# One row's load in three parts of 112, 8 and 8 partitions in a log-sum-exp kernel

## The chip, the core and the metric

The kernel runs on one core of one Trainium2 chip. A core has a matrix engine (PE), VectorE (DVE), ScalarE (ACT), GpSimd (POOL) and SyncE (SP), and 16 DMA engines that move data between the chip's main memory (HBM) and the on-chip memory of 128 partitions. The metric is the device time of one execution in microseconds (us); the number given for a kernel is the median of its runs.

## The reference

```python
def setup_inputs():
    batch, seq, dim = 32, 512, 1024
    return {"x": np.random.randn(batch, seq, dim).astype(np.float32), "axis": -1}

def reference(x, axis):
    x_max = np.max(x, axis=axis, keepdims=True)
    return (x_max.squeeze(axis) + np.log(np.sum(np.exp(x - x_max), axis=axis))).astype(np.float32)
```

For each of 32 x 512 = 16384 vectors of 1024 numbers it gives the logarithm of the sum of the exponentials. The input has 67.11 MB, the output 0.07 MB.

## The kernel before

**Tiles.** The 16384 vectors are laid out as 128 partitions with 128 vectors each: partition p holds the vectors 128p to 128p + 127. The kernel calls one vector per partition, that is 128 vectors of 4 KB, 512 KB together, a *row*; there are 128 rows. Rows are held in `ring`, a buffer of 51 rows; later rows take the places of earlier ones.

**First pass.** The exponentials are taken without subtracting the maximum. At the end the kernel checks that no sum of the rows left a safe range (`bounds`, `above`, `votes`, `verdict`, lines 283 to 312); only if one did, a second pass does the whole thing again with the maximum subtracted. With this input the second pass is not taken.

**Chunks and the order of the work.** The order is written out by hand in `CHUNKS`, a list of 17 chunks: 4, 15, 16, 16, 16, 14, 13, 9, 7, 5, 4, 3, 2, 1, 1, 1, 1 rows. Chunk `i` is loaded by `load(i)` and has its own semaphore `landed[i]`. Of each chunk, ScalarE takes the exponentials of the first `n_dve` rows in one or two instructions (line 235), and VectorE sums each row (line 255, or line 242 by halves); the other rows are done on ScalarE alone, one instruction a row, which exponentiates and sums at once (line 262, and line 225 for the last row). The last four chunks have one row each, the rows 124 to 127, all on ScalarE alone. Ahead of the last row ScalarE takes the logarithm of the sums of the rows 81 to 123 (line 162), after it that of the last four rows.

**Loads.** All loads are issued by SyncE, one after the other in the order of the chunks, onto one queue. A load waits until VectorE or ScalarE has finished with the rows of `ring` that it overwrites (`dve_wait`, `act_wait`). A load of all 128 partitions is one DMA instruction (line 155, line 146 for the last row). The waits in front of row 124 are for VectorE's sum over the rows that held its place; the loads of rows 124 to 127 are issued at 128.74, 129.12, 129.59 and 130.07 us of the profiled span, and wait in the DMA queue behind the earlier ones.

**The switch that the change uses.** `load` has a branch that splits a load by partitions. `UNEVEN` lists the chunks for which it is taken, and `PARTS` the parts: first partition, last partition, step. It is off in the kernel before (`UNEVEN` is empty). Each part adds 16 to the chunk's semaphore when it has landed, and ScalarE waits for 16 times the number of parts:

```python
nc.scalar.wait_ge(landed[i], 16 * (len(PARTS) if i in UNEVEN else 1))
```

Of the kernel before, what the change touches and what calls it, by code (L numbers as in the profile page):

```python
# [17 lines left out]
RING_ROWS = 51  # L18


UNEVEN = ()
PARTS = ((0, 128, 2), (1, 128, 4), (3, 128, 8), (7, 64, 8), (71, 128, 8))


LN_AT = 7
# [13 lines left out]
def kernel(  # L39
# [91 lines left out]
    def cuts(n, parts):  # L131
        ends = [-(-n * k // parts) for k in range(parts + 1)]
        return [(lo, hi) for lo, hi in zip(ends, ends[1:]) if lo < hi]

    def load(i):
# [8 lines left out]
        if i == len(CHUNKS) - 1:  # L144
            for k, (lo, hi) in enumerate(spans):
                nc.sync.dma_start(out=dst[:, :, lo:hi], in_=src[:, :, lo:hi]).then_inc(
                    landed[i + k], 16
                )
        elif i in UNEVEN:
            for first, last, step in PARTS:  # L150
                nc.sync.dma_start(
# [61 lines left out]
    for i, (r, n_dve, parts, by_halves) in enumerate(CHUNKS):  # L213
# [6 lines left out]
        if i == len(CHUNKS) - 1:  # L220
# [11 lines left out]
            continue  # L232
        nc.scalar.wait_ge(landed[i], 16 * (len(PARTS) if i in UNEVEN else 1))
        for lo, hi in cuts(n_dve, parts):
# [161 lines left out]
```

## Time and profile before

| | us |
|---|---|
| median of 3 runs | 162.54 |
| lowest and highest run | 162.43, 162.83 |
| the profiled execution | 162.67 |
| its span, first to last instruction | 161.3 |
| VectorE busy | 121.9 (76%) |
| ScalarE busy | 115.1 (71%) |
| mean rate of the DMA engines | 417 GB/s |

The span is what the profile's times are counted in, from the first instruction. The profile's page cuts it into 40 equal slices; a digit gives the busy share of an engine in a slice in tenths. The chain that ended last is read backwards from the last instruction, at each step to what released it. A line of the timeline gives start, duration, engine, source line, operation and shapes; where the engine stood idle before it, the idle time and what ended it follow in brackets. The issue of a DMA is an instruction of SyncE; "to landing" is the time from its issue to the last of its semaphore's counts. A load over all 16 DMA engines raises its semaphore sixteen times, once for each engine, and the trace records the time of each count.

### The profile page before, as it was taken

The page shows a single profiled execution, that of the slowest core. Times are in us where ns is not written, and L with a number is a line of the kernel's source. Part 1 is how long each engine was busy: PE and PEld are TensorE (multiplying, and loading weights), DVE is VectorE, ACT ScalarE, POOL GpSimd, SP SyncE. Part 2 cuts the span into 40 slices and gives each one's busy share as a digit, 9 for nine tenths or more (in the row PEclk, how much of TensorE's full clock was granted, in tenths as well). Part 3 has the DMA queues.
Part 4 walks back from the last instruction along what each step waited for, and adds up shares of the span by engine and source line. Part 5 has one row for each costly group of instructions (what it writes and reads, how often), then busy time and mean ns, then how long its engine had stood idle before and what let it go on. Part 6 is the DMA issues. An engine that isn't in the chain of part 4 may idle for free.

```text
span 161.3 us, 149 instructions
## 1 busy us (share of the span) xinstructions
PE 0.2 (0%) x2; PEld 0.1 (0%) x2; DVE 121.9 (76%) x51; ACT 115.1 (71%) x40; POOL 0.4 (0%) x8
## 2 busy tenths in 40 slices
PE   0000000000000000000000000000000000000000
PEld 0000000000000000000000000000000000000000
DVE  0028000003999999999999699999999999999884
ACT  3170005996079960999419993999199999999996
POOL 1000000000000000000000000000000000000000
DMA  7999799979979989989979999999999999999991
GB/s 256 508 488 442 305 472 520 439 341 520 439 341 520 423 358 520 423 358 520 423 325 455 455 455 439 423 423 423 412 402 430 436 420 410 427 436 412 417 407 42
DMA packets 2737, 67.18 MB, mean 417 GB/s; under 512 B 560, under 2 KB 560, under 8 KB 1072
## 3 DMA queue, kind: packets, MB, share of 16 engines
q1 hardware_dynamic: 2736, 67.18, 97.4%
q14 instruction: 1, 0.01, 0.0%
HBM read 67.11 MB, written 0.07 MB: 416 GB/s over the span
## 4 chain that ended last, share of the span: by engine, by line
DMA 49%; DVE 30%; ACT 20%; issue 0%; PE 0%
DMA ring<-in_x_dram 49%; DVE sums L255 29%; ACT ring L235 17%; ACT ring L262 3%; ACT ring L225 1%; ACT res L162 0%; DVE above L283 0%; PE votes L304 0%; DVE verdict L312 0%; PE votes L307 0%
## 5 line engine op out<-in xcount | busy, mean ns | idle before, releaser
L255 DVE TENSOR_REDUCE sums<-ring 128x8 f32<-128x8192 f32 (+5 forms) x14 | 111.2, 7994 | 37.3 <-ACT ring L235 37.2
L235 ACT ACTIVATE ring<-ring 128x8192 f32<-128x8192 f32 (+6 forms) x18 | 104.4, 5836 | 43.9 <-DMA ring<-in_x_dram 43.9
L242 DVE CUSTOM_DVE_ANT_0 ring<-ring 128x512 f32<-128x512 f32 x16 | 9.9, 684 | 0.0
L262 ACT ACTIVATE ring<-ring 128x1024 f32<-128x1024 f32 x8 | 8.2, 1041 | 0.0
L205 ACT ACT_TABLE_LOAD x1 | 1.3, 1283 | 0.8 <-PEq L377 0.8
L262 ACT ACTIVATION_READ_ACCUMULATOR ring<-ring 128x1 f32 x8 | 1.4, 174 | 0.0
L242 DVE DVE_READ_ACCUMULATOR2_ANT sums<- 128x1 f32 x16 | 1.3, 80 | 0.0
L225 ACT ACTIVATE ring<-ring 128x1024 f32<-128x1024 f32 x1 | 1.0, 1040 | 0.0
L283 DVE TENSOR_TENSOR above<-late,bounds 128x8 bf16<-128x8 f32 x1 | 0.2, 168 | 0.7 <-ACT res L162 0.7
L162 ACT ACTIVATE res<-sums 128x81 f32<-128x81 f32 (+1 forms) x2 | 0.5, 248 | 0.0
L312 DVE TENSOR_REDUCE verdict<-votes 1x1 int32<-1x6 f32 x1 | 0.2, 152 | 0.3 <-PE votes L307 0.3
L293 DVE TENSOR_REDUCE ends<-sums 128x1 f32<-128x124 f32 x1 | 0.3, 282 | 0.1
L304 PE MATMUL votes<-above,weights 128*1 128x6 bf16 x1 | 0.2, 167 | 160.0 <-DVE above L283 160.0
L294 DVE TENSOR_REDUCE ends<-sums 128x1 f32<-128x124 f32 x1 | 0.3, 271 | 0.0
L283 DVE TENSOR_TENSOR above<-ends,bounds 128x4 bf16<-128x4 f32 x1 | 0.2, 162 | 0.1
L162 ACT ACTIVATE res<-late 128x4 f32<-128x4 f32 x1 | 0.2, 173 | 0.0
L304 PEld LDWEIGHTS votes<-above,weights 128*1 128x1 bf16 x1 | 0.1, 80 | 160.0 <-DVE above L283 160.0
L307 PE MATMUL votes<-above,weights 128*1 128x6 bf16 x1 | 0.2, 165 | 0.0
L225 ACT ACTIVATION_READ_ACCUMULATOR ring<-ring 128x1 f32 x1 | 0.2, 153 | 0.0
L206 POOL MEMSET bounds<- 128x6 f32 x1 | 0.1, 104 | 0.4 <-POOLq L377 0.4
L207 POOL MEMSET bounds<- 128x6 f32 x1 | 0.1, 104 | 0.0
L377 POOL MEMSET const-bfloat16-1.0<- 128x1 bf16 x1 | 0.1, 103 | 0.0
(6 smaller groups left out, 0.6 us busy)
## 6 DMA issues: line engine op xcount, KB each, us to landing
ring<-in_x_dram SPq DMA_DIRECT2D x1, 7680.0 KB, 25.1
ring<-in_x_dram SPq DMA_DIRECT2D x1, 7168.0 KB, 28.6
ring<-in_x_dram SPq DMA_DIRECT2D x1, 6656.0 KB, 35.7
ring<-in_x_dram SPq DMA_DIRECT2D x1, 4608.0 KB, 20.3
ring<-in_x_dram SPq DMA_DIRECT2D x2, 2048.0 KB, 16.2
ring<-in_x_dram SPq DMA_DIRECT2D x1, 3584.0 KB, 28.5
ring<-in_x_dram SPq DMA_DIRECT2D x1, 2560.0 KB, 27.5
ring<-in_x_dram SPq DMA_DIRECT2D x4, 512.0 KB, 27.2
```

The costliest lines, as they stand in the source:

```text
L162: nc.scalar.activation(out=res[:, lo:hi], in_=src, func=Ln, bias=bias).then_inc(act_done, 1)
L205: nc.scalar.preload_act_table_set("natural_log_exp_and_others")
L225: nc.scalar.activation(out=ring[:, s, lo:hi], in_=ring[:, s, lo:hi], func=Exp, accum_out=late[:, LATE - 1 + k : LATE + k],).then_inc(act_d ...
L235: nc.scalar.activation(out=ring[:, s + lo : s + hi], in_=ring[:, s + lo : s + hi], func=Exp).then_inc(act_done, 1)
L242: nc.vector.tensor_tensor_reduce(out=ring[:, s + j, : D // 2], in0=ring[:, s + j, : D // 2], in1=ring[:, s + j, D // 2 :], scale=1.0, scal ...
L255: nc.vector.reduce_sum(out=sums[:, row + lo : row + hi], in_=ring[:, s + lo : s + hi], axis=AX).then_inc(dve_done, 1)
L262: nc.scalar.activation(out=ring[:, s + j], in_=ring[:, s + j], func=Exp, accum_out=total(row + j),).then_inc(act_done, 1)
L283: nc.vector.tensor_tensor(out=above[:, :, lo:hi], in0=values.unsqueeze(1).to_broadcast([P, 2, hi - lo]), in1=bounds[:, :, lo:hi], op=Alu.i ...
L293: nc.vector.reduce_max(out=ends[:, :1], in_=sums[:, :late_row], axis=AX).then_inc(dve_done, 1)
L294: nc.vector.tensor_reduce(out=ends[:, 1:], in_=sums[:, :late_row], axis=AX, op=Alu.min).then_inc(dve_done, 1)
L304: nc.tensor.matmul(votes[:1, :K], lhsT=weights[:, :1], rhs=above[:, 0], start=True, stop=False)
L307: nc.tensor.matmul(votes[:1, :K], lhsT=weights[:, 1:], rhs=above[:, 1], start=False, stop=True).then_inc(counted, 1)
```

## The change

The load of chunk 13, which is row 124, the fourth from last, is taken through the branch for uneven loads. It is issued as three DMA instructions instead of one: partitions 0 to 111, 112 to 119 and 120 to 127. 112 partitions are seven rows of 4 KB for each of sixteen DMA engines, and 8 partitions are one for each of eight. `PARTS`, which was not in use, gets these three parts in place of five strided ones. ScalarE's wait for this chunk is for 48 counts instead of 16. Nothing else differs: on the other engines the instructions and their order are the same.

```diff
-UNEVEN = ()
-PARTS = ((0, 128, 2), (1, 128, 4), (3, 128, 8), (7, 64, 8), (71, 128, 8))
+UNEVEN = (13,)
+PARTS = ((0, 112, 1), (112, 120, 1), (120, 128, 1))
```

## The prediction

> **What bounds the kernel now.** I read the slices of the page first, then the chain that ended last, then ScalarE's timeline over the last 15 us, then the landings of the last loads.
>
> The slices (40 equal parts of the span; the first and fourth rows are VectorE and the DMA engines):
>
> ```profile
> DVE  0028000003999999999999699999999999999884
> ACT  3170005996079960999419993999199999999996
> DMA  7999799979979989989979999999999999999991
> ```
>
> The reader should see that the DMA engines are close to full from the first slice to the last but one. The whole kernel is a stream of 67.11 MB. It ends when the last row has landed, or when ScalarE has worked off the rows before it, whichever is later. To tell which, the end of the chain is needed:
>
> ```profile
> 122.29 24.89 DMA ring<-in_x_dram
> 147.17 0.02 issue
> 147.19 2.76 ACT ring L235
> 149.96 1.04 ACT ring L262 x2
> 151.00 4.45 ACT ring L235 x2
> 155.45 3.01 ACT ring L262 x6
> 158.46 0.01 ACT res L162
> 158.47 0.03 issue
> 158.49 1.11 ACT ring L225 x2
> ```
>
> Columns: start, length, what. The last DMA in the chain is the load of four rows that lands at 147.17. From 147.19 the chain is ScalarE alone, with no landing in it, up to the last row's exponential (L225) at 158.49. ScalarE's timeline for the same stretch:
>
> ```profile
> 155.36 1.04 ACT L262 ACTIVATE ring<-ring 128x1024 f32<-128x1024 f32 x1
> ...
> 156.35 1.04 ACT L262 ACTIVATE ring<-ring 128x1024 f32<-128x1024 f32 x1
> ...
> 157.35 1.05 ACT L262 ACTIVATE ring<-ring 128x1024 f32<-128x1024 f32 x1
> ...
> 158.35 0.24 ACT L162 ACTIVATE res<-sums 128x43 f32<-128x43 f32 x1
> 158.49 1.04 ACT L225 ACTIVATE ring<-ring 128x1024 f32<-128x1024 f32 x1
> ```
>
> None of these lines has a bracket with idle time. Rows 124, 125 and 126 follow each other by 0.99 to 1.00 us. L225 follows the logarithm L162 by 0.14; the other large logarithm, 81 columns wide, is followed after 0.16 (128.09 to 128.25). So L225 started because ScalarE was free. The view of line 146, the last row's load, says how near the data was:
>
> ```profile
> L146 SPq DMA_DIRECT2D ring<-in_x_dram x1: 467/467/467, 130.1 to 130.1; - x1
> DMA to landing us min/median/max: 28.3/28.3/28.3
> ```
>
> Issued at 130.07, landed at 158.42 by the semaphore's own records, 0.07 before L225. A ScalarE instruction that did wait for a landing started 0.02 after it (147.17 to 147.19), so L225 could have started at 158.44: 0.05 us is all the slack there is. The same records put rows 124, 125 and 126 at 154.62, 155.90 and 157.18, against their exponentials at 155.36, 156.35 and 157.35: slacks of 0.74, 0.45 and 0.17. The tail is thus two chains side by side, ScalarE ahead by 0.05 us.
>
> **The change part by part.** The profiled execution took 162.67 us with a span of 161.3; the median of the three runs is 162.54. I make the sum against 162.67 and take 0.13 off at the end.
>
> *Issue on SyncE.* Row 124 is now issued by three instructions instead of one. Each issue takes 0.33 to 0.47 us (the rows at line 155 and 146), so rows 125, 126 and 127 are issued 0.75 to 0.9 later, at about 129.9, 130.4 and 130.9. Their data is first moved after 154, so 23 us of queue cover this. Without that cover it would cost the 0.9 in full. No wait is added on SyncE: the two extra pieces go with the wait of the first. ScalarE's wait for row 124 becomes 48 counts on the same semaphore, still one wait, behind which rows 125 to 127 are queued; it has the 0.74 us of slack just named. Nothing is moved past another queue, and VectorE, POOL and PE keep their order.
>
> *A row of 4 KB on one DMA engine.* One-row loads land 1.28, 1.28 and 1.24 us apart and are 8 rows on each of 16 engines, so a row takes 0.155 us. The sixteen counts of a load arrive spread out: for row 127 the first eight at 157.73 to 157.92, the others at 157.98 to 158.42. The spread is 0.67 already in the first load (6.85 to 7.52). Half of the engines run up to half a microsecond ahead for the whole kernel.
>
> *What is taken from the late half.* If the low eight engines are the early half, the late ones have 7 rows instead of 8 for row 124, which brings their last count from 158.42 to 158.26. By itself this buys nothing: L225 needs ScalarE, which is free at 158.49 by work that began at 147.19, before any of this data. The gain on the path is 0; if ScalarE were not in the way it would be 0.16.
>
> *What is given to the early half.* The low engines have two more 4 KB rows, and these come as two pieces of eight neighbouring partitions each, all eight engines writing at once. Before shows no such transfer, so I bound it. From below: the rows go at the usual pace, 2 x 0.155 = 0.31, in place of one row's 0.155, so +0.155; the first eight then end at 158.08, before the late ones. From above: the eight rows of a piece go one after the other through one path into the neighbouring partitions, 2 x 8 x 0.155 = 2.48, which is +2.33 and puts the last count at 160.25 (157.92 + 2.33). I take half of the upper end, 1.24 for both pieces, four rows queued at a time. [...] That is +1.09: the first eight end at 157.92 + 1.09 = 159.01.
>
> [...]
>
> *The 112-partition piece.* [...] Bounds: nothing, or every row shares its path with another engine's (7 x 0.155 = +1.09). I take the middle, 0.54; the late half then ends at 158.26 + 0.54 = 158.80, before 159.01, so it does not decide.
>
> *Sum.* Row 124 lands at 154.10 (its early half) + 1.09 = 155.19, still before 155.36. Row 125: 155.38 + 1.09 = 156.47, so ScalarE starts it at 156.49 instead of 156.35. Row 126: 156.66 + 1.09 = 157.75, started at 157.77 instead of 157.35; ScalarE is then free for L225 at 157.77 + 1.00 + 0.14 = 158.91. Row 127 lands at 159.01, so L225 starts at 159.03 instead of 158.49: +0.54 us. The tail after it (logarithm, comparison, matmul, verdict) is unmoved. 162.67 + 0.54 - 0.13 = 163.08, so 163.1 us, slower by 0.3%.
>
> **The rivals.**
>
> *A: the extra rows flow at the usual pace, and nothing is seen.* Landing at 158.26, ScalarE free at 158.49: change 0, so 162.5 (runs 162.43 to 162.83). For it: the engines' early lead of 0.5 us is in the records and could also hide part of the queueing; a delay of the early half up to 158.47 - 157.92 = 0.55 us costs nothing. With delays a little beyond it, or a small one in the late half, the time is 162.7 to 163.0, still no difference that can be told. [...]
>
> *B: the queueing is heavier than I took, or the low engines are not the early half.* If the extra 1.09 falls on an engine of the late half, the last landing is 158.42 + 1.09 = 159.51 and the time 162.5 + 1.05 = 163.6; with the upper end of 2.48 and early engines, 160.25 gives +1.78 and 164.3. For it: the counts carry no engine number, so nothing ties "low" to "early". Against it: an early and a late half of eight each fits a split by engine number.
>
> *C: faster, the other side.* In an execution where ScalarE gets ahead of the stream, the last landing sets the end, and one row less on the late half is worth up to 0.16 us: 162.4. It decides from the point where the last landing comes over 0.05 us later relative to ScalarE than in the profile. Even whole it is 0.1%, inside what can be told; a gain over 0.3% would need 0.49 us, which no row here offers.
>
> *D: the split does not do what it says*, for instance the 112-partition piece is spread over fewer engines. With 8 engines of 14 rows it would take 6 x 0.155 = +0.93 on these and the time would be about that of B.
>
> **How the numbers follow.** A difference of about 0.3%, 0.49 us, is what a measurement of this kernel can tell from no change. My forecast, queueing that passes 0.5 us, has 0.33; B and D, worse, 0.19; A with its small delays 0.43; C 0.05, of which 0.03 is given to over 0.3% for what I don't know. Slower 0.52, same 0.45, faster 0.03. The forecast's own range is 163.0 to 163.5. The range for 8 in 10 reaches down to A at 162.4 and up into B at 163.8; the heaviest part of B and the upper bound of the pieces are left out.
>
> **What would show it.** In the profile of the changed kernel: three issues in place of one at row 124; L225 with a DMA as its releaser in the chain and its start at 159.0; rows 125 and 126 waiting a little for landings; last counts of rows 124 to 127 late by about 0.5 against 154.62, 155.90, 157.18, 158.42. If A is right, the chain's end is that of before, with L225 0.14 after L162. If the counts' spread of 0.69 shrinks and the last comes 0.16 earlier, the balance works and only ScalarE hides it. The prediction is wrong if DMA engines queue writes without holding each other up, or if ScalarE's rows 124 to 126 start late for a reason of their own.

## The result, and the profile after

The changed kernel takes 163.25 us (median of 7 runs, 163.03 to 163.71), the kernel before 162.54 on the same chip (7 runs, 162.29 to 162.83). The ratio is 1.0052 with a 95% interval of 1.0037 to 1.0067: slower by 0.71 us by the medians, by 0.85 by the ratio, and by 0.6 to 1.1 by the interval. The profiled execution of the changed kernel is its slowest of the seven, 163.71, so part of what differs between the two profiles is not the change: the four-row load ahead of ScalarE's last stretch landed at 147.33 instead of 147.17, and the three-row load at 151.01 instead of 150.86, before any of the changed load was moved. Some 0.16 us is to be taken off each comparison.

The end of the chain, start, length and what:

```profile
130.61 27.65 DMA ring<-in_x_dram
158.26 0.02 issue
158.28 0.18 ACT ring L262
158.46 0.78 issue
159.24 0.15 ACT ring L262
159.40 0.13 ACT res L162
159.52 0.00 issue
159.53 0.03 ACT ring L225
```

Before, the last DMA in the chain was the four-row load at 147.17. Now it is the load of row 126, landed at 158.26: ScalarE no longer has a backlog, it follows the stream row by row. ScalarE's timeline:

```profile
155.71 1.06 ACT L262 ACTIVATE ring<-ring 128x1024 f32<-128x1024 f32 x1
...
157.00 1.06 ACT L262 ACTIVATE ring<-ring 128x1024 f32<-128x1024 f32 x1 [0.17 <-DMA ring<-in_x_dram]
...
158.28 1.06 ACT L262 ACTIVATE ring<-ring 128x1024 f32<-128x1024 f32 x1 [0.16 <-DMA ring<-in_x_dram]
...
159.53 1.06 ACT L225 ACTIVATE ring<-ring 128x1024 f32<-128x1024 f32 x1
```

Rows 125 and 126 now carry a bracket: ScalarE waited 0.17 and 0.16 us for their data. By the semaphores' records the rows 124 to 127 landed at 155.69, 156.98, 158.26 and 159.50; each exponential starts 0.02 or 0.03 later. The chain names the logarithm as what L225 followed, but L225 starts 0.24 after the logarithm's start where it was 0.14 before: it waited about 0.1 us for row 127. L225 starts at 159.53 instead of 158.49, later by 1.04, which is the whole difference of the two profiled executions (163.71 - 162.67).

Where the stream lost the time is seen in the DMA rate (last column, GB/s) in windows of 1 us; first the kernel before, then the changed one:

```profile
153.00:154.00 1.00, 0.00 (x0) 0.00 (x0) 0.32 (x1) 1.00 (x2) 0.00 (x0) 1.00 1.06 430
154.00:155.00 1.00, 0.00 (x0) 0.00 (x0) 1.00 (x1) 1.00 (x1) 0.00 (x0) 1.00 1.00 401
155.00:156.00 1.00, 0.00 (x0) 0.00 (x0) 1.00 (x1) 1.00 (x2) 0.00 (x0) 1.00 1.02 410
```

```profile
153.00:154.00 1.00, 0.00 (x0) 0.00 (x0) 0.16 (x1) 1.00 (x2) 0.00 (x0) 1.00 1.03 303
154.00:155.00 1.00, 0.00 (x0) 0.00 (x0) 1.00 (x1) 1.00 (x1) 0.00 (x0) 1.00 1.08 213
155.00:156.00 1.00, 0.00 (x0) 0.00 (x0) 1.00 (x1) 0.91 (x2) 0.00 (x0) 1.00 1.01 365
156.00:157.00 1.00, 0.00 (x0) 0.00 (x0) 1.00 (x1) 0.83 (x2) 0.00 (x0) 1.00 1.01 401
```

The column before the rate is the DMA engines' busy share. It stays at 1.01 to 1.08: the engines are not without work, their packets take longer. In the packet records a 4 KB packet, one partition's part of a row, takes 0.159 us before; in the changed kernel the median of those started in each half microsecond from 152.5 on is 0.17, 0.20, 0.24, 0.29, 0.38, 0.19 and then 0.16 again. Against 410 GB/s the three slow microseconds lack (107 + 197 + 45) / 410 = 0.85 us of stream.

### The profile page after: what moved, and what is told of

Its sections match the earlier page's. It is cut to its first block, busy times and chain, and to the rows that moved or that the text cites. A ratio compares the mean times of both kernels' runs of the same rounds, so it can differ in the third digit from the quotient of the medians.

```text
span 162.3 us, 151 instructions
## 1 busy us (share of the span) xinstructions
PE 0.2 (0%) x2; PEld 0.1 (0%) x2; DVE 121.9 (75%) x51; ACT 115.5 (71%) x40; POOL 0.4 (0%) x8
## 4 chain that ended last, share of the span: by engine, by line
DMA 50%; DVE 33%; ACT 13%; issue 1%; SPq 1%; PE 0%
DMA ring<-in_x_dram 50%; DVE sums L255 33%; ACT ring L235 12%; SPq L151 1%; SPq L155 0%; ACT ring L262 0%; ACT res L162 0%; ACT ring L225 0%; DVE above L283 0%; PE votes L304 0%; DVE verdict L312 0%; PE votes L307 0%
## 5 line engine op out<-in xcount | busy, mean ns | idle before, releaser
L225 ACT ACTIVATE ring<-ring 128x1024 f32<-128x1024 f32 x1 | 1.1, 1056 | 0.0
L225 ACT ACTIVATION_READ_ACCUMULATOR ring<-ring 128x1 f32 x1 | 0.2, 153 | 0.0
```

The source lines that it names most:

```text
L225: nc.scalar.activation(out=ring[:, s, lo:hi], in_=ring[:, s, lo:hi], func=Exp, accum_out=late[:, LATE - 1 + k : LATE + k],).then_inc(act_d ...
```

## The experiments

The theory, called R in the expectations: it matters which partitions a load takes, and the parts of some loads queue. What R says of the reason (the shares, and which engine writes into which partitions) is the author's assumption; no run shows it. Its rivals: O, each further DMA instruction costs something; B, the number of rows per engine (nine and seven, or low engines that are not early) decides. One more rival is not tested by any run: partition p always takes the vectors 128p to 128p + 127, so a load that writes other partitions also reads other places of HBM. The runs can show that it matters which partitions a load takes; whether the limit lies where they are written, as R says, or where they are read, they cannot tell apart.

Low, in the prediction, the expectations and the table, are the engines that a load of eight partitions goes to; high are the others. What the semaphores' records show is sixteen counts for a load of 128 or of 112 partitions and eight late ones for a load of eight. They carry no engine number: that every load of eight goes to the same eight engines is assumed, and the rows per engine are counted from the partitions on that assumption.

The diffs are against the kernel before and show the new lines that matter; lines for semaphores and waits are left out, and so is `UNEVEN = (13,)` where only `PARTS` is shown.

Beside the time I use one figure from the semaphores' records: the stretch from the last count of the three-row load (chunk 11) to the last count of row 127. It leaves out how early or late the stream is in an execution. It is 158.42 - 150.86 = 7.56 us before and 159.50 - 151.01 = 8.49 in the changed kernel: +0.93. It comes from one execution of each kernel. Three kernels whose last loads are all whole (the one before and the last two described below) have 7.55 to 7.56, so a difference of 0.1 us counts.

| kernel | rows per engine in row 124 | time to before (95%) | stretch, us |
|---|---|---|---|
| before | 8 | | 7.56 |
| changed: 112, 8, 8 | 9 low, 7 high | 1.0052 (1.0037 to 1.0067) | 8.49 |
| three column parts | 8 | 1.0011 (1.0000 to 1.0022) | 7.70 |
| two halves | 8 | 1.0090 (1.0076 to 1.0103) | 9.12 |
| even and odd | 8 | 1.0000 (0.9991 to 1.0009) | 7.58 |
| 112 and 16 | 8 | 1.0083 (1.0069 to 1.0096) | 8.58 |
| five strided parts | 9 low, 7 high | 1.0008 (0.9998 to 1.0018) | 7.85 |
| whole, and 2 x 8 neighbours again | 10 low, 8 high | 1.0040 (1.0026 to 1.0054) | 8.31 |
| whole, and 2 x 8 spread again | 10 low, 8 high | 1.0020 (1.0010 to 1.0030) | 7.85 |
| whole, and 128 again | 16 | 1.0077 (1.0061 to 1.0092) | 8.85 |
| whole, and 112 again | 15 | 1.0125 (1.0107 to 1.0143) | 9.49 |

**Three loads by columns.**

```diff
+UNEVEN = (13,)
+PARTS = ((0, 512), (512, 768), (768, 1024))
...
+            for lo, hi in PARTS:
+                nc.sync.dma_start(out=dst[:, :, lo:hi], in_=src[:, :, lo:hi]).then_inc(
```

> Row 124 comes in three loads again, but each over all 128 partitions and a part of the columns (512, 256, 256). Every DMA engine has its usual partitions and the same bytes as before; only the number of DMA instructions and of counts is that of the changed kernel. Theory R (the rows write into destinations that no longer match one engine each, and queue there): no change, 162.5, at most +0.1 for the shorter packets. Theory O (each further DMA costs something of its own on the queue): +0.6 to +0.8 as in the changed kernel, 163.2. Theory B (the count of rows per engine decides): no change.

162.73 (11 runs) against 162.46 (21 runs): 0.1% slower, the interval just touching no change, and a stretch longer by 0.14. Three DMA instructions, their counts and the shorter packets are worth about that. O would have needed 0.93, and it falls.

**Two halves, and even and odd.** The same number of DMAs, the same four rows per engine in each, other destinations:

```diff
+PARTS = ((0, 64, 1), (64, 128, 1))     # two halves
+PARTS = ((0, 128, 2), (1, 128, 2))     # even and odd
```

> Row 124 comes in two loads, partitions 0 to 63 and 64 to 127: four rows for each of sixteen engines in each load, so eight in all, as before. Theory R: sixteen engines write into half of the receiving side at a time; if a half takes half the rate, each load needs 8 x 0.155 = 1.24 us instead of 0.62, the stream loses 1.24 us and the time is about 162.5 + 1.2 = 163.7. Theory B: rows per engine are equal, no change, 162.5. Theory O: one DMA more instead of two, about +0.35, 162.9.

> Row 124 comes in two loads, the even and the odd partitions: the same number of DMAs and of rows per engine as with two halves, only the destinations of each load reach over all partitions. Theory R: clearly less than with halves, between no change and +0.6 (162.5 to 163.1), since the shares are evenly filled over a load but two engines can meet in one. Theories B and O: the same as with halves.

The halves cost 1.39 us (163.85 against 162.46), even and odd nothing (162.45). The rates of the two kernels, halves first:

```profile
152.50:153.50 1.00, 0.00 (x0) 0.00 (x0) 0.20 (x1) 0.77 (x1) 0.00 (x0) 1.00 1.08 221
153.50:154.50 1.00, 0.00 (x0) 0.00 (x0) 1.00 (x1) 0.86 (x1) 0.00 (x0) 1.00 1.01 234
154.50:155.50 1.00, 0.00 (x0) 0.00 (x0) 1.00 (x1) 1.00 (x1) 0.00 (x0) 1.00 0.97 254
```

```profile
152.50:153.50 1.00, 0.00 (x0) 0.00 (x0) 0.13 (x1) 1.00 (x2) 0.00 (x0) 1.00 1.01 406
153.50:154.50 1.00, 0.00 (x0) 0.00 (x0) 1.00 (x1) 1.00 (x1) 0.00 (x0) 1.00 1.02 410
154.50:155.50 1.00, 0.00 (x0) 0.00 (x0) 1.00 (x1) 1.00 (x2) 0.00 (x0) 1.00 1.05 418
```

The reader should see 221 to 254 GB/s against 406 to 418, with the engines busy in both. This is the clearest pair: nothing but which partitions a load takes differs. The rate depends on the partitions: half of them, taken as a block, got 54 to 61% of the rate of even and odd in the windows shown (221 against 406, 234 against 410, 254 against 418). The loss over the whole stretch is more than the 1.24 us that R worked out from half the rate: 9.12 - 7.56 = 1.56 us; why was not shown. Even and odd was foreseen to cost something, up to 0.6; it cost nothing.

**112 and 16.** The balance taken away, the 112 kept:

```diff
+PARTS = ((0, 112, 1), (112, 128, 1))
```

> Row 124 comes in two loads, partitions 0 to 111 and 112 to 127: seven rows and one row for each of sixteen engines, so the balance is eight for all, as before. Theory R: the 112-partition load costs what it costs in the changed kernel (about 0.3 us), and the 16 neighbouring partitions, written by sixteen engines at once, another 0.47 (four queued, 0.62 instead of 0.155): +0.5 to +0.8, about 163.2. Theory B (nine rows on engines that are not early is what costs): no change, 162.5.

163.72 against 162.46: every engine has its eight rows by the count, and it is not cheaper than nine and seven. B, the balance alone as the cause, falls with this run. The size foreseen, 0.5 to 0.8, was too small: 1.26 by the medians, 1.1 to 1.6 by the interval.

**Five strided parts.** Nine and seven again by the count, with the destinations apart:

```diff
+UNEVEN = (13,)
 PARTS = ((0, 128, 2), (1, 128, 4), (3, 128, 8), (7, 64, 8), (71, 128, 8))
```

> Row 124 comes in the five strided parts that stood unused in the kernel before: 64, 32, 16, 8 and 8 partitions, again nine rows for each of the low eight engines and seven for the others. Theory R: each part reaches over many shares, so less than the changed kernel: +0.1 to +0.5, 162.6 to 163.0. Theory B (nine and seven is what costs): +0.7 as the changed kernel. Theory O: four more DMAs instead of two, +1.4, 163.9.

162.69 against 162.62, not to be told from no change, where nine and seven in three blocks cost 0.5%. The stretch is longer by 0.29, so it is not free on the stream, and with five instructions it speaks against O once more.

**The small pieces by themselves.** Row 124 whole, then two pieces of eight partitions once more into a free row that is not read:

```diff
+EXTRA = ((112, 120, 1), (120, 128, 1))   # neighbours
+EXTRA = ((64, 96, 4), (65, 97, 4))       # spread
...
+            if i == 13:
+                for first, last, step in EXTRA:
+                    nc.sync.dma_start(
+                        out=ring[first:last:step, 34:35], in_=src[first:last:step]
+                    ).then_inc(landed[i], 16)
```

> Row 124 is loaded whole as before, and then two pieces of eight neighbouring partitions (112 to 119, 120 to 127) are loaded a second time into a free row of the ring, where nobody reads them; ScalarE waits for them all the same. This is the pieces' cost without the 112-partition load: the low eight engines have ten rows, the others eight. Theory R: the pieces take 2 x 4 x 0.155 = 1.24 us on the low engines, less their lead of 0.5: +0.6 to +0.8, about 163.2. Theory B, with low engines early: 2 x 0.155 = 0.31, hidden by the lead, no change; with low engines late: +0.31, 162.8.

> As the run with two extra pieces, but the eight partitions of each piece are four apart (64, 68, ... 92 and 65, 69, ... 93). Engines and bytes are the same, only the destinations are apart. Theory R: each of the eight rows goes to a place of its own, so the pieces cost about 0.31 on the low engines and as much on the engines that they meet there: 0 to +0.3, 162.5 to 162.8, and clearly less than with neighbouring partitions. Theory B: the same time as with neighbouring partitions.

163.28 with neighbours, 163.03 with spread partitions, 162.62 before; the stretches are longer by 0.75 and 0.29. The number of partitions and the bytes are the same, so the difference of 0.46 us of stream goes with which partitions the pieces take. The rate in the microsecond of the pieces, neighbours and then spread:

```profile
154.00:155.00 1.00, 0.00 (x0) 0.00 (x0) 1.00 (x1) 1.00 (x1) 0.00 (x0) 1.00 0.89 184
```

```profile
154.00:155.00 1.00, 0.00 (x0) 0.00 (x0) 0.96 (x1) 1.00 (x2) 0.00 (x0) 1.00 1.05 295
```

By the median the spread pieces cost 0.41 us, more than the 0 to 0.3 that I gave them (0.2 to 0.5 by the interval). Why was not shown.

In the run with neighbours all sixteen counts of row 127 come later than any did before: 158.46 to 159.13 against 157.73 to 158.42, though the four-row load had landed at the same time (147.16 and 147.17). A piece of eight partitions leaves eight late counts in the records, so it is moved by eight engines. The engines without a piece were thus held up as well, by at least 0.04 us and, if the order is kept, by about as much as the others. R, as the expectation has it, delays the low engines alone; what holds up all sixteen is open.

**The 112 by itself.** Row 124 whole, then once more into the free row, all of it or partitions 0 to 111:

```diff
+EXTRA = ((0, 128, 1),)
+EXTRA = ((0, 112, 1),)
```

> Row 124 is loaded whole as before and then whole a second time into a free row of the ring, where nobody reads it; ScalarE waits for both. This is the price of 512 KB on the stream when every engine keeps its usual partitions. All theories: the last landing moves by one row's 1.28 us, the time by 1.2, to about 163.75. It is the measure for the run with 112 partitions.

> As the run with a second whole load, but the second load has the partitions 0 to 111 only: an eighth less data, seven rows of 4 KB for each engine. If only bytes and rows per engine count, it is cheaper than the whole second load by 0.155 us: 163.6. [...]

163.80 and 164.60: the smaller load is dearer by 0.80 us. By the stretch it is 9.49 against 8.85, 0.64 more with 0.155 us less to move, so the 112-partition load alone loses about 0.8 us. That is more than the 0.3 to 0.5 that the author had estimated for it from the slow stretch of the changed kernel (163.9 to 164.1). The rates while the second load runs, 128 first, then 112:

```profile
154.00:155.00 1.00, 0.00 (x0) 0.00 (x0) 1.00 (x1) 1.00 (x1) 0.00 (x0) 1.00 1.03 410
155.00:156.00 1.00, 0.00 (x0) 0.00 (x0) 1.00 (x1) 0.51 (x2) 0.00 (x0) 1.00 1.03 410
156.00:157.00 1.00, 0.00 (x0) 0.00 (x0) 1.00 (x2) 0.94 (x2) 0.00 (x0) 1.00 1.02 406
```

```profile
154.00:155.00 1.00, 0.00 (x0) 0.00 (x0) 1.00 (x1) 1.00 (x1) 0.00 (x0) 1.00 1.04 303
155.00:156.00 1.00, 0.00 (x0) 0.00 (x0) 1.00 (x1) 0.55 (x1) 0.00 (x0) 1.00 1.04 266
156.00:157.00 1.00, 0.00 (x0) 0.00 (x0) 1.00 (x1) 0.19 (x1) 0.00 (x0) 1.00 0.98 336
```

The 128-partition load runs at the usual rate, the 112-partition load at 266 to 336 GB/s.

**Twice the bytes.** The same three parts for the chunk before, of two rows:

```diff
+UNEVEN = (12,)
+PARTS = ((0, 112, 1), (112, 120, 1), (120, 128, 1))
```

> The three parts of 112, 8 and 8 partitions are used for the chunk before, which has two rows of the ring: the same three DMAs with twice the bytes. Theory R: the loss grows with the bytes, 2 x 0.8 us of stream, +1.5, about 164.0. Theory O: +0.7 as in the changed kernel, 163.2. Theory B: two rows' imbalance of 0.31, hidden by the lead or +0.3.

165.01 against 162.62, ratio 1.0146 (1.0124 to 1.0167). From the last count of the four-row load to that of row 127 it takes 160.67 - 147.17 = 13.50 us instead of 158.42 - 147.17 = 11.25, a loss of 2.25 and thus more than twice 0.93. A cost that grows with the bytes is what R says; a cost per DMA would have stayed. The size was missed: R had +1.5 and about 164.0, measured was +2.39 by the medians, and why the loss more than doubles is not known.

**Are the low engines the early ones?** A transfer of 64 bytes for each of eight partitions behind row 124:

```diff
+            if i == 13:
+                nc.sync.dma_start(
+                    out=ring[64:96:4, 34:35, :16], in_=src[64:96:4, :, :16]
+                ).then_inc(landed[-1], 16)
```

> Behind the whole load of row 124 goes a transfer of 64 bytes for each of eight partitions, on a semaphore of its own; its late counts come from the eight low engines, each as soon as that engine is through with row 124. If the low engines are the early half, the eight counts fall together with the first eight counts of row 124 (within some 0.25 us, ahead of the others); if low engines stand anywhere in the order, they spread over the whole 0.7 us. The time should be that of before.

The eight late counts come at 153.74 to 154.20, those of row 124 at 153.52 to 154.39. In the packet records each 64-byte packet begins 6 ns after its engine's count for row 124 began, which gives the engine's place: among the sixteen count records for row 124, the low engines hold the places 1, 2, 3, 4, 5, 7, 8 and 11. So low is mostly early, seven of the first eight, but not cleanly. The one execution took 162.55, as before.

**The split at the start of the stream.** If the lead is there from the first load, it could be evened out there, so that the landing that starts ScalarE's last stretch comes earlier too:

```diff
+            if i == 0:
+                nc.sync.dma_start(out=dst[:, :2], in_=src[:, :2]).then_inc(landed[i], 16)
+                for first, last, step in PARTS:
+                    nc.sync.dma_start(
+                        out=dst[first:last:step, 2:], in_=src[first:last:step, 2:]
+                    ).then_inc(landed[i], 16)
+                return
```

> The uneven split at the other end of the stream: of the first chunk's four rows two are loaded whole and two in the five strided parts, nine to seven, and row 124 is whole again. If the low engines are ahead from the start and keep their lead, they get 2 x 0.155 us more and the others as much less, the spread of the counts shrinks from 0.67 to some 0.1 to 0.3, all later landings come 0.15 to 0.3 earlier, the one that starts ScalarE's last stretch (147.17 before) too, and the time falls to 162.2 to 162.4. If the strided parts cost what they gain, or the low engines are not early, no change or +0.2.

163.70 against 162.56, ratio 1.0064 (1.0046 to 1.0082): neither of the two outcomes written down. The stretch at the end is that of before (159.84 - 152.29 = 7.55), so the loss is at the start: the first chunk landed at 9.49 instead of 7.52, the four-row load at 148.60 instead of 147.17. The counts' spread for row 127 grew to 1.08 us (158.76 to 159.84). The issues of this kernel, start and length:

```profile
0.45 3.20 SPq L158 DMA_DIRECT2D ring<-in_x_dram  x5
...
4.40 1.28 SPq L162 DMA_DIRECT2D ring<-in_x_dram  x3
```

The five issues hold SyncE until 3.65, and the next loads are issued from 4.40 on instead of 0.80. By the packet records only 13 to 14 of the 16 engines are busy on average between 6.5 and 7.5. Some engines run dry before the next load reaches them. How much of the loss is that and how much is queueing was not separated.

No kernel here is faster than the one before; even and odd equals it.

## Why the prediction was right

163.25 was measured for a forecast of 163.1, slower, and the stream did lose time because of the partitions that the three parts take, as the forecast had it. That the number came so close is partly luck: the loss was laid on half of the engines, where all sixteen were late, and two terms were off in opposite directions. Step by step:

- *What bounds the end.* Two chains side by side, ScalarE ahead by 0.05 us, was the right reading. With 0.93 us lost on the stream and 0.05 of slack, L225 should come 0.88 later; it came 1.04 later in an execution whose stream was 0.16 late already. (In the slices shown there the DMA engines are the third row, not the fourth.)
- *Issue on SyncE at no cost.* Right: rows 125 to 127 were issued at 130.21, 130.61 and 131.09, and they landed 26.8 to 28.4 us later. The delay was 1.0 to 1.1 us instead of 0.75 to 0.9; 0.35 of it is that the first part was itself issued later, at 129.09 instead of 128.74.
- *What is taken from the late half buys nothing.* The gain was 0 on the path, but for another reason as well: the late engines were not relieved. Taking off the stream's earlier lateness (0.24 for the first count, 0.16 for the last), the first count of row 127 came 1.00 later and its last 0.92 later. Both halves lost about the same. The spread shrank only from 0.69 to 0.53.
- *The two pieces, +1.09 on the low engines.* The kind was right: the pieces without the 112 stretch the stream by 0.75, spread pieces by 0.29. No run shows 1.24 us for the two pieces, or four rows queued at a time; nor does any show which partitions an engine writes in a whole load. Two pieces of 1.24 us, less the lead of about 0.5, would give 0.74, next to the 0.75 measured, but that match is luck: the sum delays the low engines alone, and in that run all sixteen were late. The premise that the low engines have half a microsecond to spare held for most of them.
- *The 112-partition piece, 0.54, not deciding.* No run shows the 0.54, the middle of two bounds, or rows of two engines on one path. This is the term that was mis-sized. By itself it loses about 0.8 us, as much as the pieces. My sum had the late half end 0.38 late (158.80) and the early half deciding at 0.59 (159.01); measured, the last count is 0.92 late, net of the earlier lateness. The sum also has a gap: it puts the 0.54 on the late half alone, though the early engines carry seven rows of the same piece. With both terms on them the early half would end at 157.92 + 0.54 + 1.09 = 159.55 and the time would be about 163.6, outside the forecast's own range of 163.0 to 163.5. The 0.54 was too small and was left out for half of the engines, and the pieces cost less beside the 112 than I gave them: these errors partly cancel.
- *Row 124 without a wait.* Wrong by size: I had it land at 155.19, before ScalarE asks for it. It landed at 155.69, 0.91 later net of the same 0.16, and ScalarE started it at 155.71; its instruction ahead had ended at 155.62, a wait too short for a bracket.
- *The sum*, +0.54, against +0.71 by the medians: the two losses do not add up (0.8 and 0.75 alone, 0.93 together). Why was not shown.
- *The signs named beforehand.* Three issues at row 124 and short waits of rows 125 and 126 (0.17 and 0.16) are there. The last counts were 0.9 late, not 0.5, and L225 started at 159.53, not 159.0. The chain does not name a DMA as what released L225.
- *The rivals.* A, nothing seen, fell: the lead does not cover 0.93. B, heavier queueing, gave 163.6 and was too much for the median. C did not show. D, fewer engines for the 112, falls: in the run where the 112 is loaded by itself behind the whole row, sixteen counts come for it at 155.53 to 156.78 and none at its issue, while a piece of eight partitions leaves one record at its issue and eight late ones.

## What to carry to other kernels

The rate of this full stream depended on which partitions each load takes. From 152.5 to 155.5 loads over all of them kept 397 to 422 GB/s (before), loads over every second one 406 to 418, and blocks of half of them fell to 221 to 254, by the count with the same number of rows on every engine. Why is not shown. Before rows are shifted from late to early engines, look at which partitions the shifted rows go to, and at whether the late engines end the path at all; here an intended gain of 0.16 us, hidden behind ScalarE, stood against a loss of 0.93. A lead of some engines at the end of a long stream can be seen in the spread of a load's semaphore counts, here 0.69 us for row 127 before.

## What the hardware showed that was not expected

A load of 112 partitions is slower than one of 128: 0.64 us more of stream for an eighth less data. Two loads of every second partition cost nothing that can be told (ratio 1.0000, 0.9991 to 1.0009), though by the count each has four rows per engine as the halves have. And in all these slow stretches the DMA engines' busy share stays near 1 (0.88 to 1.12): a busy DMA engine is not one that moves data at its rate, so the GB/s column is the one to read.
